# A pool of 160 bytes and a gap of 192 bytes that move the weights and the tokens to another distance in SBUF

## The chip, the cores and the metric

The kernel runs on one core of one Trainium2 chip. The metric is the device time of one execution in microseconds (us). Before the change it is 1328.35 us, the median of three runs (1327.24 to 1328.72).

## What is computed

One layer of a streaming encoder for 288 tokens (256 of a prompt and 32 of a running stream, D_MODEL 2048), all in float32:

```
xn   = rmsnorm(x);  proj = xn @ w_in               # 2048 x 5664
pool = trailing means of u_pool, times w_pool      # 4 groups of 256 x 256
ssd  = SSD mixer (conv, chunked scan, gate, norm)
x    = x + rmsnorm(concat[pool, ssd] @ w_out)      # 3072 x 2048
h    = rmsnorm(x) @ w_up                           # 2048 x 11264
f    = silu(conv(gate)) * conv(value)
x    = x + rmsnorm(f @ w_down)                     # 5632 x 2048
```

The new states of the mixers and of the convolutions are outputs too.

## The kernel before, in words

**Products.** Weights are the stationary operand, tokens the moving one. Both are split into a high and a low float32r part. A block of 128 x 128 weights with one token tile takes three matmuls, in `mm3` (lines 141 to 144): high weights with high tokens (L142), high weights with low tokens (L143), low weights with high tokens (L144). Each has 288 moving columns, and each is preceded by a load of its weights. One "product" below is one such load and matmul, a "triple" the three of `mm3`.

**Token tiles.** A token tile is `[128, 2, 288]` float32r: per partition 1152 bytes of high part, then 1152 bytes of low part. 1152 is 4 x 256 + 128, so the low part lies at 128 bytes (mod 256) from the high part, and one tile of 2304 bytes is 9 x 256, so all tiles of a pool have the same address mod 256.

**Weights.** `project` (L146) runs a stage: `fetch_w` (L117) issues the DMA of up to 1 MB into a `raw` tile of `wpool`, `split_w` (L124) makes `whi` on ScalarE (L136) and `wlo` on VectorE (L137), 4096 bytes each per partition, also in `wpool`. A weight block begins at a multiple of 512 bytes within them, so all weights of `wpool` have one address mod 256. The first stage alone (`prepare`, L270 and L359) has its split weights in a tile `w` of the pool `xin`.

**The stages**, in the order of time, and the token tiles that they read:

| stage | us of the span | token tile, pool | triples |
|---|---|---|---|
| first part of w_in (L359) | 4 to 39 | `xn`, apool | 96 |
| rest of w_in | 47 to 310 | `xn`, apool | 608 |
| w_pool | 296 to 333 | `du`, outp | 16 |
| w_out, SSD part | 312 to 456 | `mixs`, apool | 256 |
| w_out, pool part | 340 to 469 | `mixp0` to `mixp7`, outp | 128 |
| w_up, both halves | 475 to 755, 897 to 1176 | `hn`, apool | 1408 |
| w_down, both halves | 756 to 897, 1176 to 1299 | `fa`, ffn | 660 |
| last 256 columns of w_down (L1262, L1263, L1285) | 1299 to 1318 | `fa`, ffn | other shapes |

In between stand a few small products: the sums over features (L690, L891: the weights are the tile `ones_r` of ones), the SSD heads (L631 to L637), the new states (L972, L973, 512 columns).

**Pools.** Tile pools are laid out in SBUF one behind the other in the order in which they are opened: const, wpool, apool, bpool, upool, and behind these xin, then mixer, then outp, then ffn, each in the place of the one that was closed. Every tile is rounded up to 32 bytes per partition.

**Order.** The scheduler sets the order of the instructions on each engine from its own estimates; many are pinned to the program's order.

Of the kernel before, what the change touches and what calls it, by code (L numbers as in the profile page):

```python
# [8 lines left out]
F32 = mybir.dt.float32  # L9
# [7 lines left out]
P = 128  # L17
# [8 lines left out]
HEADS = 32  # L26
# [4 lines left out]
NF = D_FF // P  # L31
# [19 lines left out]
)  # L51
SUMS_AT = 11
TURN_AT = 13
NEAR = 8


@with_exitstack
def body(
# [24 lines left out]

    const = ctx.enter_context(tc.tile_pool(name="const", bufs=1))
    wpool = ctx.enter_context(tc.tile_pool(name="wpool", bufs=4))
    apool = ctx.enter_context(tc.tile_pool(name="apool", bufs=16))
    bpool = ctx.enter_context(tc.tile_pool(name="bpool", bufs=20))
    acc_ps = ctx.enter_context(tc.tile_pool(name="acc_ps", bufs=5, space=PSUM))
# [135 lines left out]
    first_load(9)  # L224
    cols = const.tile([P, sum(n for _, n in COLS)], F32, name="cols")
    pin(sp.dma_start(out=cols, in_=cols_in))
    hp = const.tile([HEADS, 3], F32, name="hp")
    pin(sp.dma_start(out=hp, in_=heads_in))
    col = {}
    for name, n in COLS:  # L230
# [2 lines left out]

    ones = const.tile([P, P], F32, name="ones")
    pool.memset(ones, 1.0)
    eps_t = const.tile([P, 1], F32, name="eps_t")
    pool.memset(eps_t, EPS)
    warm = const.tile([P, 1], F32, name="warm")
    pin(act.activation(warm, eps_t, AF.Copy))
    ident = const.tile([P, P], F32, name="ident")  # L240
    make_identity(nc, ident)
# [1 line left out]
    pool.affine_select(  # L243
        out=tri, in_=ones, pattern=[[1, P]], compare_op=ALU.is_ge, fill=0.0, base=0, channel_multiplier=-1
    )
    rec = const.tile([P, 16], F32, name="rec")
    for t in range(16):
        pool.memset(rec[:, t : t + 1], 1.0 / (t + 1))
    scan_one = const.tile([HEADS, NT], F32, name="scan_one")
# [224 lines left out]
    def htile(name, n=NT, tag=None):  # L474
        return mp.tile([HEADS, n], F32, tag=tag or name, name=name, bufs={"z": 4}.get(tag, 2) if tag else 1)
# [23 lines left out]
    r = htile("r", tag="z")  # L499
# [355 lines left out]

    xT = op_.tile([P, NEAR, NT], F32, name="xT2")
    x1 = []
# [146 lines left out]
    for grp in ((0, 1), (2,), (3,), (4,), (5,), (6, 7)):  # L1004
# [13 lines left out]
        if grp[0] == 0:  # L1018
            sp.dma_start(out=xT.rearrange("p k n -> p (k n)"), in_=x_g[:, KD : KD + NEAR * NT])
            sp.dma_start(out=new_sconv, in_=sc_stage.rearrange("p s r t -> p (s r t)"))  # L1020
# [15 lines left out]
    def hn_of(t):  # L1036

        a = atile("hn")
        hi = act.activation(a[:, 0, :], x1[t], AF.Copy, scale=g_ffn_pre[:, t : t + 1])  # L1039
        lo = pin(dve.scalar_tensor_tensor(  # L1040
            a[:, 1, :], x1[t], g_ffn_pre[:, t : t + 1], a[:, 0, :].bitcast(F32),
            op0=ALU.mult, op1=ALU.subtract,
        ))
        if t == 0:
            late.extend((hi, lo))
        q = xsum if t == 0 else op_.tile([P, NT], F32, tag="sq", bufs=2, name="sq")
        act.activation(q, x1[t], AF.Square)
        hn.append(a)
        if t == 1:
            state_out(*still)  # L1050
        if t:
            squares[t] = q
        if t > 1:
            pin(dve.tensor_tensor(xsum, xsum, squares.pop(t - 1), op=ALU.add))

    todo = list(range(KD))
    for s in range(KD):
        pin(dve.tensor_tensor(x1[s], x1[s], rm, op=ALU.mult))
        if s < NEAR:
            pin(dve.tensor_tensor(x1[s], x1[s], xT[:, s, :], op=ALU.add))  # L1060
        else:
            pin(pool.dma_start(out=x1[s], in_=x_g[:, KD + NT * s : KD + NT * (s + 1)], accum_op=ALU.add))
        while todo and todo[0] + (1 if todo[0] < NEAR else NEAR) <= s:
            hn_of(todo.pop(0))
# [9 lines left out]

    ffn = ExitStack()
    fp = ffn.enter_context(tc.tile_pool(name="ffn", bufs=1))
    fc_stage = fp.tile([P, 2, 2, 2 * NF], F32, name="fc_stage")
    nconv = [0]

    def fconv(i, p_):  # L1080
# [79 lines left out]
    for q in range(4):  # L1160
        for b in range(2):
            t = apool.tile([P, 512], F32, tag="a", name="xr")
# [31 lines left out]
    def factors(src, bias, n, name):  # L1194
        o = const.tile([P, 2], F32, tag="trs", bufs=2, name=name)[:, :n]
        pin(act.activation(o, src, AF.Sqrt, bias=bias, scale=1.0 / D_MODEL))
        pin(dve.reciprocal(o, o))
        return o
# [53 lines left out]
    def turn(t):  # L1252
        c = slice((t - A) * P, (t - A + 1) * P)
        pin(pe.transpose(last[:, 2 * P + c.start : 2 * P + c.stop], part[t][:, P:NP_], ident))
        pin(pe.matmul(last_s[P - NS :, c], part[t][:, NP_:], ident, start=True, stop=True))
# [27 lines left out]
    for k, hi, lo in sum(parts, []):  # L1283
# [4 lines left out]
        if k == SUMS_AT:  # L1288
            other_sums(sq[0], False)
            rf = factors(p_f, eps_t, 2, "rf1")  # L1290
        if k == TURN_AT:
            turn(A)
# [108 lines left out]
```

## Time and profile before

| what | value |
|---|---|
| median of 3 runs | 1328.35 us |
| the profiled execution, its own time | 1328.16 us |
| its span, first to last instruction | 1326.4 us |
| granted TensorE clock | 1.000 |
| DVE (VectorE), ACT (ScalarE), POOL (GpSimd) busy | 67%, 51%, 19% |
| largest DMA group, w_up | 80 of 1 MB, 5.1 us to landing |

How to read it: the page gives for each engine the busy share of the span, then the chain of work that ended last, then groups of instructions. Matmuls overlap in the record: a product of 288 columns is shown with about 295 ns, but the next one starts about 132 ns later. So the pace is read from starts, or from the number of products in a stretch. The stretches of the windows view count every instruction that touches the stretch, the two or so that were under way at its start among them.

### The profile page before, as it was taken

The page shows a single profiled execution, that of the slowest core. Times are in us where ns is not written, and L with a number is a line of the kernel's source. Part 1 is how long each engine was busy: PE and PEld are TensorE (multiplying, and loading weights), DVE is VectorE, ACT ScalarE, POOL GpSimd, SP SyncE. Part 2 cuts the span into 40 slices and gives each one's busy share as a digit, 9 for nine tenths or more (in the row PEclk, how much of TensorE's full clock was granted, in tenths as well). Part 3 has the DMA queues.
Part 4 walks back from the last instruction along what each step waited for, and adds up shares of the span by engine and source line. Part 5 has one row for each costly group of instructions (what it writes and reads, how often), then busy time and mean ns, then how long its engine had stood idle before and what let it go on. Part 6 is the DMA issues. An engine that isn't in the chain of part 4 may idle for free.

```text
span 1326.4 us, 25268 instructions
## 1 busy us (share of the span) xinstructions
PE 1319.0 (99%) x10043; PEld 1307.9 (99%) x10043; DVE 894.3 (67%) x1515; ACT 672.5 (51%) x1013; POOL 247.5 (19%) x399
## 2 busy tenths in 40 slices
PE   9999999999999999999999999999999999999998
PEld 9999999999999999999999999999999999999997
DVE  7999987879645688876766743336666666654454
ACT  7557767446543567544444433334444454444442
POOL 2342222222232231211211200001111111101110
PEclk9999999999999999999999999999999999999999
DMA  8578875456566478666455444545444544466653
GB/s 340 183 216 280 280 215 177 155 169 208 198 210 223 138 196 264 198 176 205 160 162 175 157 161 165 164 166 180 167 159 162 178 169 160 162 231 181 209 177 114
DMA packets 110038, 251.75 MB, mean 190 GB/s; under 512 B 64736, under 2 KB 73856, under 8 KB 87392
## 3 DMA queue, kind: packets, MB, share of 16 engines
q1 hardware_dynamic: 103424, 233.22, 54.2%
q0 software_dynamic: 5824, 16.13, 4.2%
q8 instruction: 78, 1.28, 0.4%
q10 hardware_dynamic: 672, 0.80, 0.2%
q14 instruction: 40, 0.33, 0.1%
HBM read 237.11 MB, written 13.00 MB: 189 GB/s over the span
## 4 chain that ended last, share of the span: by engine, by line
PE 98%; DMA 0%; ACT 0%; DVE 0%; issue 0%; ACTq 0%
PE acc L142 30%; PE acc L144 30%; PE acc L143 30%; PE acc L359 2%; PE acc_x L359 1%; PE py L631 1%; PE acc L1262 0%; DMA xg<-in_x_g 0%; PE acc L1263 0%; PE acc_t L1285 0%; PE acc_x L143 0%; PE acc_x L142 0%; PE acc_x L144 0%; PE py L633 0%; PE pst L972 0%; PE acc L366 0%
## 5 line engine op out<-in xcount | busy, mean ns | idle before, releaser
L137 DVE TENSOR_TENSOR wlo<-raw,whi 128x1024 fp32r<-128x1024 f32 (+1 forms) x396 | 472.8, 1195 | 321.0 <-ACT whi L136 319.2
L136 ACT ACTIVATE whi<-raw 128x1024 fp32r<-128x1024 f32 (+1 forms) x396 | 408.3, 1033 | 486.2 <-PE acc L143 401.3
L142 PE MATMUL acc<-hn,whi 128*128 128x288 f32 x1376 | 404.6, 296 | 0.5 <-ACT hn L1039 0.4
L143 PE MATMUL acc<-hn,whi 128*128 128x288 f32 x1376 | 403.4, 294 | 0.0
L144 PE MATMUL acc<-hn,wlo 128*128 128x288 f32 x1376 | 403.0, 294 | 0.0
L143 PEld LDWEIGHTS acc<-hn,whi 128*128 128x128 f32 x1376 | 259.7, 189 | 0.1
L144 PEld LDWEIGHTS acc<-hn,wlo 128*128 128x128 f32 x1376 | 259.5, 189 | 0.0
L142 PEld LDWEIGHTS acc<-hn,whi 128*128 128x128 f32 x1376 | 257.2, 187 | 1.4 <-ACT hn L1039 0.8
L143 PE MATMUL acc<-fa,whi 128*128 128x288 f32 x660 | 195.4, 296 | 0.0
L142 PE MATMUL acc<-fa,whi 128*128 128x288 f32 x660 | 195.3, 296 | 0.0
L144 PE MATMUL acc<-fa,wlo 128*128 128x288 f32 x660 | 195.0, 295 | 0.0
L142 PE MATMUL acc<-xn,whi 128*128 128x288 f32 x608 | 180.1, 296 | 0.0
L144 PE MATMUL acc<-xn,wlo 128*128 128x288 f32 x608 | 178.8, 294 | 0.0
L143 PE MATMUL acc<-xn,whi 128*128 128x288 f32 x608 | 178.8, 294 | 0.0
L143 PEld LDWEIGHTS acc<-fa,whi 128*128 128x128 f32 x660 | 124.4, 188 | 0.0
L142 PEld LDWEIGHTS acc<-fa,whi 128*128 128x128 f32 x660 | 124.0, 188 | 0.0
L144 PEld LDWEIGHTS acc<-fa,wlo 128*128 128x128 f32 x660 | 123.8, 188 | 0.0
L1088 POOL COPY fc_stage<-ebuf 128x4 f32<-128x4 f32 x88 | 26.7, 304 | 483.7 <-DVE ebuf L1087 462.2
L143 PEld LDWEIGHTS acc<-xn,whi 128*128 128x128 f32 x608 | 114.9, 189 | 0.0
L144 PEld LDWEIGHTS acc<-xn,wlo 128*128 128x128 f32 x608 | 114.7, 189 | 0.1
L142 PEld LDWEIGHTS acc<-xn,whi 128*128 128x128 f32 x608 | 113.9, 187 | 0.7 <-issue 0.5
L1094 DVE SCALAR_TENSOR_TENSOR fc<-ebuf,cols,fc 128x290 f32<-128x290 f32 x176 | 90.1, 516 | 3.7 <-ACT fc L1092 1.0
(338 smaller groups left out, 1778.4 us busy)
## 6 DMA issues: line engine op xcount, KB each, us to landing
raw<-in_w_up SPq DMA_DIRECT2D x80, 1024.0 KB, 5.1
raw<-in_w_in SPq DMA_DIRECT2D x38, 1024.0 KB, 5.2
raw<-in_w_down SPq DMA_DIRECT2D x32, 1024.0 KB, 5.0
raw<-in_w_out SPq DMA_DIRECT2D x24, 1024.0 KB, 5.1
raw<-in_w_down SPq DMA_DIRECT2D x16, 768.0 KB, 4.4
raw<-in_w_up SPq DMA_DIRECT2D x14, 512.0 KB, 4.1
gb<-g_d POOLq DMA_DIRECT2D x8, 832.0 KB, 6.0
raw<-in_w_first SPq DMA_DIRECT2D x5, 768.0 KB, 12.6
```

The source lines that it names most:

```text
L136: act.activation(hi, raw[:, k : k + n, :], AF.Copy)
L137: dve.tensor_tensor(lo, raw[:, k : k + n, :], hi.bitcast(F32), op=ALU.subtract)
L142: then(pe.matmul(out, wh, a[:, 0, :], start=start, stop=False))
L143: then(pe.matmul(out, wh, a[:, 1, :], start=False, stop=False))
L144: then(pe.matmul(out, wl, a[:, 0, :], start=False, stop=stop))
L359: pin(pe.matmul(first[m], w[:, k, r * NB + m * P :][:, :P], xn[kb + k][:, x, :], start=kb + k + r + x == 0, stop=kb + k == KD - 1 and r == ...
L631: ins = pe.matmul(y[c, 0:256], xw[:, 0, f_], m[:, h, 0:256], start=True, stop=False)
L1088: pool.tensor_copy(fc_stage[:, :, :, i], e[:, 256:324].rearrange("p (s c) -> p s c", c=34)[:, :, 0:2])
L1094: dve.scalar_tensor_tensor(c, e[:, r_ : r_ + 290], f_w[:, r_, i : i + 1], c, op0=ALU.mult, op1=ALU.add)
```

## The change

Four small tiles (`hp`, `eps_t`, `warm`, `rec`; 32 + 32 + 32 + 64 = 160 bytes with the rounding) leave the pool `const`, which lies ahead of `wpool`, for a new pool `side`, which lies behind it and ahead of `apool`. And `fc_stage`, the first tile of the pool `ffn`, becomes the front part of a tile that is 48 floats (192 bytes) longer.

```diff
+FC_GAP = 48
...
     wpool = ctx.enter_context(tc.tile_pool(name="wpool", bufs=4))
+    side = ctx.enter_context(tc.tile_pool(name="side", bufs=1))
     apool = ctx.enter_context(tc.tile_pool(name="apool", bufs=16))
...
-    hp = const.tile([HEADS, 3], F32, name="hp")
+    hp = side.tile([HEADS, 3], F32, name="hp")
...
-    eps_t = const.tile([P, 1], F32, name="eps_t")
+    eps_t = side.tile([P, 1], F32, name="eps_t")
...
-    warm = const.tile([P, 1], F32, name="warm")
+    warm = side.tile([P, 1], F32, name="warm")
...
-    rec = const.tile([P, 16], F32, name="rec")
+    rec = side.tile([P, 16], F32, name="rec")
...
-    fc_stage = fp.tile([P, 2, 2, 2 * NF], F32, name="fc_stage")
+    fc_room = fp.tile([P, 8 * NF + FC_GAP], F32, name="fc_stage")
+    fc_stage = fc_room[:, : 8 * NF].rearrange("p (s r t) -> p s r t", s=2, r=2)
```

Both programs have the same instructions in the same order on every engine; they differ in addresses. `wpool` begins 160 bytes earlier, at 34624 instead of 34784; apool, bpool, upool, xin, mixer and outp stay where they were; what lies behind `fc_stage` in ffn begins 192 bytes later. Addresses in SBUF mod 256, and the distance token minus weight (high part / low part):

| stage | weights, before / after | tokens, before / after | distance before | distance after |
|---|---|---|---|---|
| first part of w_in | 160 / 160 | 224 / 224 | 64 / 192 | 64 / 192 |
| rest of w_in, w_pool, w_out SSD part, w_up | 224 / 64 | 224 / 224 | 0 / 128 | 160 / 32 |
| w_out, mixp0 to mixp3 | 224 / 64 | 96 / 96 | 128 / 0 | 32 / 160 |
| w_out, mixp4 to mixp7 | 224 / 64 | 224 / 224 | 0 / 128 | 160 / 32 |
| w_down | 224 / 64 | 32 / 224 | 64 / 192 | 160 / 32 |

`ones_r`, in const behind the tiles that left, moves from 64 to 160; the tokens of L891 lie at 96 and 224 in both.

## The prediction

> **What bounds the kernel now.** First the page: its busy shares, its clock row and its chain of work.
>
> ```profile
> span 1326.4 us, 25268 instructions
> PE 1319.0 (99%) x10043; PEld 1307.9 (99%) x10043; DVE 894.3 (67%) x1515; ACT 672.5 (51%) x1013; POOL 247.5 (19%) x399
> ...
> PEclk9999999999999999999999999999999999999999
> ...
> PE 98%; DMA 0%; ACT 0%; DVE 0%; issue 0%; ACTq 0%
> PE acc L142 30%; PE acc L144 30%; PE acc L143 30%; PE acc L359 2%; PE acc_x L359 1%; PE py L631 1%; PE acc L1262 0%; DMA xg<-in_x_g 0%; PE acc L1263 0%; PE acc_t L1285 0%; PE acc_x L143 0%; PE acc_x L142 0%; PE acc_x L144 0%; PE py L633 0%; PE pst L972 0%; PE acc L366 0%
> ```
>
> TensorE is busy for 99% of the span at the full granted clock, and 98% of the chain that ended last is TensorE, nine tenths of it in the three lines of `mm3`. Then the view of waits, for TensorE; its two longest entries:
>
> ```profile
> PE acc_x L265 <- DVE busy L192: 1.3, 1, 1.3
> PE acc L359 <- ACT w L294: 0.7, 1, 0.7
> ```
>
> Nobody keeps it waiting. The order of instructions is the same in both programs, so only one thing can move the time: how long a product takes from its start to the next start. The durations of single matmuls (295 ns) overlap, so I count products in long stretches that hold one stage each: the windows view, with the stretch, then TensorE's busy time and its instructions.
>
> ```profile
> core 0: us, PE busy (x) PEld busy (x) DVE busy (x) ACT busy (x) POOL busy (x), PEclk, DMA share, GB/s
> ...
> 50.00:105.00 55.00, 55.00 (x418) 55.00 (x418) 53.91 (x121) 28.09 (x42) 24.16 (x24) 1.00 0.62 186
> 560.00:740.00 180.00, 180.00 (x1363) 180.00 (x1362) 123.21 (x221) 84.57 (x114) 30.29 (x56) 1.00 0.55 173
> 760.00:890.00 130.00, 130.00 (x977) 130.00 (x976) 51.20 (x50) 48.17 (x61) 1.20 (x1) 1.00 0.51 169
> 900.00:1170.00 270.00, 270.00 (x2044) 270.00 (x2043) 178.31 (x313) 126.67 (x170) 47.53 (x82) 1.00 0.50 166
> ```
>
> About 2.2 products were under way at the start of a stretch (295 ns over 132). Without them w_in (50 to 105) gives 55,000/415.8 = 132.3 ns per product, w_up 180,000/1360.8 = 132.3 and 270,000/2041.8 = 132.2, w_down 130,000/974.8 = 133.4. The shape is the same everywhere. DVE is busy for 98% of the w_in stretch and 39% of the w_down one, and yet w_down is the slower: the load beside TensorE isn't the cause. What differs is the distance between tokens and weights: 0/128 bytes in w_in and w_up, 64/192 in w_down. I use 132.25 and 133.35.
>
> **Is it the distance, or the place of the tokens alone?** The first part of w_in has its tokens where the rest of w_in has them (224), and weights at 160: distance 64/192. The timeline, with start, length, line and count:
>
> ```profile
> 28.93 1.76 PE L359 MATMUL acc_x<-xn,w 128*128 128x288 f32 x12
> 30.53 3.36 PE L359 MATMUL acc<-xn,w 128*128 128x288 f32 x24
> 33.73 1.76 PE L359 MATMUL acc_x<-xn,w 128*128 128x288 f32 x12
> ```
>
> From 28.93 to 33.73 stand 36 products: 4.80/36 = 133.3 ns, the pace of w_down to the last digit, with tokens and weights both at other addresses than there. So the distance sets it. The third distance in this kernel is 128/0, at mixp0 to mixp3. Two of the eight passages over these tiles, from the second triple to the end, 21 products each:
>
> ```profile
> 347.24 0.30 PE L142 MATMUL acc<-mixp,whi 128*128 128x288 f32 x1
> ...
> 349.99 0.29 PE L142 MATMUL acc<-mixp,whi 128*128 128x288 f32 x1
> ```
> ```profile
> 386.91 0.30 PE L142 MATMUL acc<-mixp,whi 128*128 128x288 f32 x1
> ...
> 389.69 0.29 PE L142 MATMUL acc<-mixp,whi 128*128 128x288 f32 x1
> ```
>
> 2.75/21 = 131.0 ns, and 2.78/21 = 132.4. Seven passages go like the first and one like the second: the pace is one of a few fixed ones, and what came before can decide which.
>
> **A rule of the skill that speaks against the change.** The rows above differ by 2.4 ns with the distance. The Trainium skill, page "TensorE: Matmul & The Clock Gate", section "Step-by-step: what each phase is for", says that TensorE has two independent read ports into SBUF, so that loading the next weights takes nothing from the running matmul. By that the distance would be without effect and the sum zero; the rows of w_in and L359 differ from it in the small, by 0.8%.
>
> **The change part by part.** *What is removed and added:* no instruction. *What moves:* `wpool` by 160 bytes, `fa` by 192. The split of weights reads and writes inside `wpool` alone, so its operands keep their distances; its two instructions end ahead of TensorE's need (the waits above name neither), and I cost them at nothing. The covers are DVE's idle time, which is 1.1 us of 55 in the stretch 50 to 105. A TensorE faster by 1% would meet DVE there at 99%; if it bound, up to 0.5 us of the gain of that stretch would be lost. The landing address of the weights' DMA moves as well; they land here in 5.1 us:
>
> ```profile
> raw<-in_w_up SPq DMA_DIRECT2D x80, 1024.0 KB, 5.1
> ```
>
> One such MB is two splits' worth of weights and feeds 48 products (6.3 us), and no wait of TensorE names a DMA: nothing.
>
> *The main products.* Their counts, from the page and from the groups kept apart by shape:
>
> ```profile
> L142 PE MATMUL acc<-hn,whi 128*128 128x288 f32 x1376 | 404.6, 296 | 0.5 <-ACT hn L1039 0.4
> ...
> L142 PE MATMUL acc<-fa,whi 128*128 128x288 f32 x660 | 195.3, 296 | 0.0
> ...
> L142 PE MATMUL acc<-xn,whi 128*128 128x288 f32 x608 | 180.1, 296 | 0.0
> ```
> ```profile
> L142 PE MATMUL acc<-mixs,whi 128*128 128x288 f32 x256 | 75.4, 295 | 0.0
> ...
> L142 PE MATMUL acc<-mixp,whi 128*128 128x288 f32 x128 | 37.8, 295 | 0.0
> ...
> L142 PE MATMUL acc_x<-hn,whi 128*128 128x288 f32 x32 | 9.1, 295 | 0.0
> ```
>
> From distance 0/128 to 160/32 go hn 1408, xn 608, mixs 256, half of mixp 64 and w_pool 16 triples: 2352, or 7056 products. From 64/192 to 160/32 go fa's 660 triples, 1980 products. From 128/0 to 32/160 go the other 64 of mixp, 192 products.
>
> *The pace at 160/32* stands in no long stretch. The bounds, by rows: the fewest nanoseconds are those of L1285, 256 columns.
>
> ```profile
> 1312.78 2.22 PE L1285 MATMUL acc_t<-whi,fa 128*128 128x256 f32 x18
> ```
>
> 18 products span 2.22 us, the last one alone some 0.28: 1.94/17 = 114 ns, or 128.5 for 288 columns if it went by columns. The most are those just behind a run of 512 columns, with distance 0/128:
>
> ```profile
> 373.78 0.30 PE L142 MATMUL acc<-mixs,whi 128*128 128x288 f32 x1
> ...
> 374.19 0.30 PE L142 MATMUL acc<-mixs,whi 128*128 128x288 f32 x1
> ```
>
> 0.41/3 = 136.7 ns. Only four products have weights and tokens at 32 and 160 now, the sums of L891, and they too follow on 512 columns:
>
> ```profile
> 470.09 0.29 PE L891 MATMUL psum_m<-mhi,ones_r 128*128 128x288 f32 x1
> 470.22 0.29 PE L891 MATMUL psum_m<-mlo,ones_r 128*128 128x288 f32 x1
> 470.36 0.30 PE L891 MATMUL psum_m<-mhi,ones_r 128*128 128x288 f32 x1
> 470.49 0.35 PE L891 MATMUL psum_m<-mlo,ones_r 128*128 128x288 f32 x1
> ```
>
> Three starts in 0.40 us, 133 ns, against the 0.41 us of distance 0/128 in the same position. The starts are rounded to 0.01 us, so this says little: not worse than 0/128, and no sign of 128. In the circle of 256 bytes, two of three products of a triple go to 160, which is 32 from 128 (the best row, 131.0) and 96 from 0 and from 64. I take the nearest row, **131.0**.
>
> Sum: 7056 x (132.25 - 131.0) = 8.8 us; 1980 x (133.35 - 131.0) = 4.7 us; the 192 products of mixp0 to mixp3 go the other way, to 32, between 0 and 64, at (132.25 + 133.35)/2 = 132.8: 192 x 1.8 = 0.35 us lost. The last 132 products of w_down have other shapes; at 1 to 2 ns each they are 0.2 us, left out. Together 13.1 us less. From the profiled execution's 1328.16 us that gives 1315.1, and the median stands 0.2 above it: **1315 us**, 1.0% less.
>
> **The rivals.**
>
> *Slower: 160 behaves as 64 does.* Then all stages go at the pace of w_down: 7056 x 1.1 = 7.8 us more, 192 x 2.35 = 0.45 more, 1336.6. For it: two of the four distances seen pairwise (64 and 192) are bad, the weights now begin at another place within 64 bytes than the tokens, which no long stretch shows, and L891 gave 133. Against: 160 lies nearer to 128. It decides from a pace of (7056 x 132.25 + 1980 x 133.35 + 192 x 131.0)/9228 = 132.5 ns on: above that the change loses.
>
> *No effect, or 160 behaves as 0.* If the distance has no part in it, 1328. If 160 is as 0, only w_down gains, 1980 x 1.1 = 2.2 us: 1326. For it: the best distance, 128, went at 132.4 in one passage, as 0 does. Its first half is the skill's rule above; the rows of L359 speak against that half.
>
> *Much faster: 160 avoids what all three others still pay.* At the lower bound, 128.5: 7056 x 3.75 + 1980 x 4.85 + 192 x 2.5 = 36.5 us less, 1292. For it: one step of 64 bytes moves the pace by 1 ns already, and none of the three distances is an odd multiple of 32. Against: L891.
>
> **How the numbers follow.** Nearest row, 1309 to 1322: 0.34. Much faster, down to 1292: 0.24. No effect or as 0, 1323 to 1330: 0.14. Slower, 1331 and above: 0.28, mostly up to 1337; beyond that only if 160 is worse than all that is seen (136.7 would be some 40 us more). Below 1292 and above 1337 I leave 0.05 and 0.12, so the range is 1292 to 1337. A measurement of this kernel tells about 0.2% (2.7 us) from no change. Faster by more: 0.34 + 0.24 and a little of the third case, 0.60. Within 0.2%: 0.13. Slower: 0.27.
>
> **What would show it.** In the windows view of the changed kernel the stretches inside w_up and w_down must have the same pace now, both having 160/32: at 131.0 ns 180 us hold 1376 products, against 1363. If they are equal but at 133, the slower rival is right; if w_down keeps a pace of its own, it isn't the distance that set it. L359 keeps 64/192 and must keep its 133.3. The chain stays TensorE's; a wait of TensorE for `whi` or `wlo` between 50 and 105 us would show that DVE's cover is gone. All of it is wrong if the pace depends on which cycle a stage falls into at its start rather than on the distance: then equal distances would show unequal paces.

## The result

| | before | changed |
|---|---|---|
| median of 5 runs each | 1328.35 us | 1322.35 us (1321.8 to 1322.48) |
| ratio, with 95% interval | | 0.9955 [0.9940, 0.9969] |
| profiled execution, own time | 1328.16 us | 1322.35 us |
| its span | 1326.4 us | 1320.6 us |

The kernel became 6.0 us faster (0.45%). The forecast was 13.1 us (1315), with a range of 1292 to 1337. The sign holds; the size is less than half. After the change the page reads as before: the same instructions, TensorE busy throughout at the full clock, and the chain of work nine tenths in the three lines of `mm3` (now L144 to L146). Only the head of the chain differs: up to 38.7 us it goes over the DMA and the split of the first weights, where it went over L359 before.

```profile
span 1320.6 us, 25268 instructions
PE 1313.9 (99%) x10043; PEld 1302.5 (99%) x10043; DVE 894.7 (68%) x1515; ACT 672.5 (51%) x1013; POOL 251.8 (19%) x399
...
PEclk9999999999999999999999999999999999999999
...
PE 96%; DMA 1%; DVE 1%; ACT 1%; issue 0%; SPq 0%; ACTq 0%
```

In the view of waits TensorE's list still names neither `whi` nor `wlo`; its longest three entries:

```profile
PE acc_x L267 <- DVE busy L194: 1.3, 1, 1.3
PE py__15330 L1330 <- ACT diag L1329: 0.7, 1, 0.7
PE acc L144 <- ACT hn L1041: 0.4, 1, 0.4
```

The windows view of the changed kernel, the same stretches as in the prediction:

```profile
50.00:105.00 55.00, 55.00 (x419) 55.00 (x418) 53.99 (x122) 28.47 (x41) 24.97 (x24) 1.00 0.63 186
560.00:740.00 180.00, 180.00 (x1367) 180.00 (x1366) 122.67 (x221) 84.92 (x113) 33.36 (x56) 1.00 0.56 175
760.00:890.00 130.00, 130.00 (x988) 130.00 (x987) 50.79 (x48) 48.81 (x60) 0.00 (x0) 1.00 0.50 167
900.00:1170.00 270.00, 270.00 (x2050) 270.00 (x2049) 178.93 (x314) 126.78 (x170) 47.48 (x82) 1.00 0.51 169
```

Less the 2.2 that were under way, w_up ran 1364.8 products in 180 us (131.9 ns each; before 132.3) and w_down 985.8 in 130 us (131.9; before 133.4). The two stages have one pace now, but the stretch from 560 to 740 shows 1367 products where 131.0 ns would have shown 1376. The first part of w_in, whose distance didn't change, stands in the timeline:

```profile
32.87 1.76 PE L361 MATMUL acc_x<-xn,w 128*128 128x288 f32 x12
34.47 2.70 PE L361 MATMUL acc<-xn,w 128*128 128x288 f32 x19
```

12 products from 32.87 to 34.47: 1.60/12 = 133.3 ns, as before.

Counts in a window are good to one product. Where more digits are given below, the pace is the time between the starts of the first and the last product of an unbroken stretch of the trace, over their number. By that measure the 5.8 us of the span come from:

| products | distance | ns per product, before to after | us |
|---|---|---|---|
| w_up (hn), 4224 | 0/128 to 160/32 | 132.23 to 131.85 | -1.6 |
| w_in, rest (xn), 1824 | 0/128 to 160/32 | 132.25 to 131.94 | -0.6 |
| w_out, mixs, 768 | 0/128 to 160/32 | 132.33 to 131.50 | -0.6 |
| w_out, mixp4 to mixp7, 192 | 0/128 to 160/32 | 132.21 to 131.24 | -0.2 |
| w_out, mixp0 to mixp3, 192 | 128/0 to 32/160 | 131.37 to 133.31 | +0.4 |
| w_down (fa), 1980 | 64/192 to 160/32 | 133.33 to 131.86 | -2.9 |

Together -5.5 us. The first part of w_in, with the same distance, ends 0.3 us earlier; that is inside the scatter of the program's head, since the rest of w_in begins anywhere from 46.4 to 48.2 us in the kept traces. The middle rows already hold a question: mixs and w_up have the same distances, 160/32, and not the same pace.

### The profile page after: what moved, and what is told of

Same layout as the page of the kernel before. It is cut to its first block, busy times and chain, and to the rows that moved or that the text cites. A ratio compares the mean times of both kernels' runs of the same rounds, so it can differ in the third digit from the quotient of the medians.

```text
span 1320.6 us, 25268 instructions
## 1 busy us (share of the span) xinstructions
PE 1313.9 (99%) x10043; PEld 1302.5 (99%) x10043; DVE 894.7 (68%) x1515; ACT 672.5 (51%) x1013; POOL 251.8 (19%) x399
## 4 chain that ended last, share of the span: by engine, by line
PE 96%; DMA 1%; DVE 1%; ACT 1%; issue 0%; SPq 0%; ACTq 0%
PE acc L145 30%; PE acc L144 30%; PE acc L146 30%; DMA raw<-in_w_first 1%; PE py L633 1%; PE acc L1265 0%; DVE w L300 0%; PE acc L1266 0%; PE acc_t L1288 0%; PE acc_x L145 0%; PE acc_x L144 0%; PE acc_x L146 0%; DVE sq L320 0%; PE py L635 0%; PE acc L361 0%; PE acc_x L361 0%
## 5 line engine op out<-in xcount | busy, mean ns | idle before, releaser
L146 PE MATMUL acc<-hn,wlo 128*128 128x288 f32 x1376 | 404.5, 295 | 0.0
L144 PE MATMUL acc<-hn,whi 128*128 128x288 f32 x1376 | 402.9, 294 | 0.5 <-ACT hn L1041 0.4
L144 PEld LDWEIGHTS acc<-hn,whi 128*128 128x128 f32 x1376 | 258.8, 189 | 1.4 <-ACT hn L1041 0.8
L146 PEld LDWEIGHTS acc<-hn,wlo 128*128 128x128 f32 x1376 | 258.3, 188 | 0.0
L146 PE MATMUL acc<-fa,wlo 128*128 128x288 f32 x660 | 194.6, 295 | 0.0
L144 PE MATMUL acc<-fa,whi 128*128 128x288 f32 x660 | 194.0, 294 | 0.0
L146 PE MATMUL acc<-xn,wlo 128*128 128x288 f32 x608 | 179.5, 296 | 0.0
L144 PE MATMUL acc<-xn,whi 128*128 128x288 f32 x608 | 179.4, 295 | 0.0
L144 PEld LDWEIGHTS acc<-fa,whi 128*128 128x128 f32 x660 | 124.5, 189 | 0.0
L146 PEld LDWEIGHTS acc<-fa,wlo 128*128 128x128 f32 x660 | 123.9, 188 | 0.0
L144 PEld LDWEIGHTS acc<-xn,whi 128*128 128x128 f32 x608 | 114.6, 189 | 0.7 <-issue 0.5
L146 PEld LDWEIGHTS acc<-xn,wlo 128*128 128x128 f32 x608 | 114.2, 188 | 0.1
L1086 POOL COPY ebuf<-cols 128x2 f32<-128x2 f32 x88 | 74.0, 842 | 108.7 <-DVE fc L1097 61.2
```

What stands on the lines that cost most here:

```text
L144: then(pe.matmul(out, wh, a[:, 0, :], start=start, stop=False))
L146: then(pe.matmul(out, wl, a[:, 0, :], start=False, stop=stop))
L1086: pool.tensor_copy(e[:, 258:260], hist_f[:, :, i])
```

## Experiments

### One part of the change at a time, and the place without the distance

Theory "distance": only the distance between tokens and weights (mod 256) counts. Rival "place": the address of the weights or of the tokens alone counts. `side_only` is the change without the gap in `fc_stage` (w_down then lies at 224/96); `gap_only` is the gap without the side pool (w_down then lies at 0/128 and all else as before).

> The side pool alone, no gap in ffn: w_in, w_out and w_up at distance 160/32 (weights at 64 mod 256), w_down at 224/96, a pair not seen yet. Theory 'distance' (the pace depends on token minus weight mod 256): w_up at 131.85 ns per product as after the change, which is 7056 x 0.4 = 2.8 us less than before; w_down anywhere from 130 to 134 ns, a pace of its own: 1325.5 us with up to 7 us either way. Theory 'place' (it is the weights' own address, 64 instead of 224, that helps): w_down at 131.85 as well, 1322.4 us.

> The gap alone, no side pool: weights at 224, w_down at distance 0/128, everything else as before. Theory 'distance': w_down takes the pace of w_up, 132.25 instead of 133.35 ns, 1980 x 1.1 = 2.2 us less: 1326.2 us. Theory 'place' (the weights' own address): nothing changes, 133.35 ns in w_down and 1328.35 us.

`abs96` puts 96 bytes in front of everything: weights and tokens move together, no distance changes, and the weights begin at 64 as in the changed kernel.

```diff
+    const.tile([P, 24], F32, name="gap")
```

> 96 bytes at the head of the pool const: weights at 64 mod 256 as after the change, but the tokens move with them, so all distances are those of before (0/128 and 64/192). Theory 'distance': 132.25 ns in w_up, 133.35 in w_down, 1328.35 us. Theory 'place': w_up and w_down at 131.85, 1322.4 us.

`pad128` puts 128 bytes between `wpool` and `apool`: 128/0 for w_in and w_up, 192/64 for w_down. It asks whether the 131.0 ns of the prediction's row at 128/0 hold in a long stage.

```diff
     wpool = ctx.enter_context(tc.tile_pool(name="wpool", bufs=4))
+    gap = ctx.enter_context(tc.tile_pool(name="gap", bufs=1))
+    gap.tile([P, 32], F32, name="gap")
```

> 128 bytes between wpool and apool: w_in, w_out and w_up at 128/0, w_down at 192/64. This is the row that the prediction took for the pace, in a whole stage. If the seven fast passages over mixp0 to mixp3 are the rule: 131.0 ns in w_up, 7056 x 1.25 = 8.8 us less, 1319.5 us if w_down keeps its pace. If a long stage settles in the cycle of the eighth passage: 132.4 ns in w_up, about 1 us more, 1329.4 us. w_down at 192/64 is open, 131 to 134 ns.

| kernel | us (runs) | ratio to before | w_up | w_down |
|---|---|---|---|---|
| side_only | 1323.75 (6) | 0.9971 [0.9959, 0.9983] | 160/32: 131.85 | 224/96: 133.33, then 132.23 |
| gap_only | 1325.74 (10) | 0.9985 [0.9976, 0.9995] | 0/128: 132.22 | 0/128: 132.22 |
| abs96 | 1327.37 (10) | 0.9998 [0.9988, 1.0007] | 0/128: 132.23 | 64/192: 133.33 |
| pad128 | 1325.22 (10) | 0.9979 [0.9970, 0.9989] | 128/0: 132.22 | 192/64: 132.59 |

One stretch of w_up and one of w_down in the windows view of each; first `abs96`:

```profile
560.00:740.00 180.00, 180.00 (x1364) 180.00 (x1363) 122.89 (x221) 85.05 (x113) 31.21 (x56) 1.00 0.55 173
770.00:880.00 110.00, 110.00 (x827) 110.00 (x826) 43.01 (x38) 41.87 (x52) 0.00 (x0) 1.00 0.50 168
```

1364 and 827 products; the kernel before has 1363 and 827 in these stretches. The place alone does nothing, and "place" falls. `gap_only`:

```profile
560.00:740.00 180.00, 180.00 (x1363) 180.00 (x1362) 122.57 (x221) 85.11 (x113) 32.51 (x56) 1.00 0.56 173
770.00:880.00 110.00, 110.00 (x834) 110.00 (x833) 43.39 (x38) 42.22 (x53) 0.00 (x0) 1.00 0.50 169
```

Only w_down changed, to 834 - 2.2 products in 110 us, 132.2 ns: the pace that w_up has at the same 0/128. `side_only`, with a second stretch of w_down:

```profile
560.00:740.00 180.00, 180.00 (x1367) 180.00 (x1366) 123.23 (x222) 85.10 (x114) 33.36 (x57) 1.00 0.56 176
770.00:880.00 110.00, 110.00 (x827) 110.00 (x826) 43.40 (x38) 41.57 (x52) 0.00 (x0) 1.00 0.50 168
...
1190.00:1285.00 95.00, 95.00 (x720) 95.00 (x720) 47.16 (x56) 42.06 (x57) 12.64 (x11) 1.00 0.66 197
```

w_up has the pace of the changed kernel without the gap. But w_down runs its first half at 133.4 ns (824.8 products in 110 us) and its second at 132.4 (717.8 in 95 us), with the same distance 224/96. So the distance doesn't name one pace; it allows some. `pad128` shows the same thing in w_in. Its group of first products in the window from 60 to 95 us, then w_up:

```profile
L144 PE MATMUL acc<-xn,whi 128*128 128x288 f32 x90 | 26.6, 295 | 0.0
```
```profile
59.91 0.30 PE L144 MATMUL acc<-xn,whi 128*128 128x288 f32 x1
...
94.92 0.29 PE L144 MATMUL acc<-xn,whi 128*128 128x288 f32 x1
```
```profile
560.00:740.00 180.00, 180.00 (x1363) 180.00 (x1363) 122.78 (x221) 85.01 (x113) 30.91 (x56) 1.00 0.55 172
```

90 triples from 59.91 to 94.92 are 89 x 3 products in 35.01 us: 131.1 ns. The interruption of the stream by small products at 106 to 109 us ends that: behind it the triples (from the start of one to the start of the next, read from the trace in ns) go 395, 398, 395, 399, which is 132.2 ns a product; another interruption, at 199 us, brings 389, 397, 394 back. And w_up, at the same 128/0, runs 1360.8 products in 180 us, 132.3 ns, to its end. The row that the prediction rested on is thus one of two paces of 128/0, and the time of `pad128` lies between the two that were expected.

### High and low tokens by themselves

Theory "own": the pace of a triple is the sum of what each product's own distance costs. In these kernels all three products of `mm3` read the high tokens, or all three the low ones, so that a stage has one distance only (half of the tokens' parts is left out, so what they compute isn't the layer); `pure_0` and `pure_128` stand on the kernel before, `pure_160` and `pure_32` on `side_only`.

```diff
-        then(pe.matmul(out, wh, a[:, 1, :], start=False, stop=False))
+        then(pe.matmul(out, wh, a[:, 0, :], start=False, stop=False))
```
```diff
-        then(pe.matmul(out, wh, a[:, 0, :], start=start, stop=False))
+        then(pe.matmul(out, wh, a[:, 1, :], start=start, stop=False))
...
-        then(pe.matmul(out, wl, a[:, 0, :], start=False, stop=stop))
+        then(pe.matmul(out, wl, a[:, 1, :], start=False, stop=stop))
```

> The layout of before, but the second product of every triple reads the high part of the tokens again: the low part is left out of the result, and all three products have one distance, 0 in w_in, w_out and w_up, 64 in w_down. Theory 'own' (each product pays for its own distance, and a triple is the sum): from the pairs seen so far, 0/128 at 396.7 ns per triple and 128/0 at 396.7, 64/192 at 400 and 192/64 at 397.8, follow 132.2 ns per product for 0 and 134.1 for 64. Theory 'cycle' (the stream of loads and products falls into one of a few fixed cycles that the distances allow, and no product has a price of its own): any of the paces seen, 131.1 to 133.3, and no need to be 134.1 at 64.

> The layout of before with the low part of the tokens in all three products (the high part is left out of the result): distance 128 alone in w_in, w_out and w_up, 192 alone in w_down. 'Own': 132.2 ns for 128 and 131.85 for 192. 'Cycle': 131.1 or 132.2 for 128, 192 open.

> The side pool without the gap, high part of the tokens in all three products (the low part is left out of the result): distance 160 alone in w_in, w_out and w_up, 224 alone in w_down. 'Own': from 160/32 at 395.6 and 32/160 at 399.9 ns per triple follow 130.4 ns for 160, the best of all. 'Cycle': one of 131.1 or 131.85 again. 224 alone: open, as the pair 224/96 went at 133.3 in one half and 132.2 in the other.

> The side pool without the gap, low part of the tokens in all three products (the high part is left out of the result): distance 32 alone in w_in, w_out and w_up, 96 alone in w_down. 'Own': 134.8 ns for 32; for 96 from 224/96 somewhere in 131 to 136. 'Cycle': 131 to 133.3 for both.

One profiled run each, 1320.84, 1335.82, 1334.62 and 1333.04 us beside 1327.82 before. w_up in the windows views of `pure_0`, `pure_160` and `pure_32`:

```profile
560.00:740.00 180.00, 180.00 (x1369) 180.00 (x1369) 123.52 (x223) 85.36 (x115) 32.07 (x57) 1.00 0.56 175
```
```profile
560.00:740.00 180.00, 180.00 (x1353) 180.00 (x1352) 122.65 (x222) 84.28 (x112) 32.76 (x57) 1.00 0.56 174
```
```profile
560.00:740.00 180.00, 180.00 (x1353) 180.00 (x1352) 123.51 (x225) 85.01 (x114) 30.98 (x56) 1.00 0.56 173
```

0 alone runs at 131.7 ns; 160 alone and 32 alone both run at 133.3 (1350.8 products in 180 us), and yet 160 and 32 by turns run at 131.85. "Own", which wanted 130.4 for 160 alone, falls: what counts is how the distances follow on one another. By starts, the others alone: 64 at 132.22 or 131.67, 96 at 131.67, and 128, 192 and 224 at 133.33.

### The other distances

`pad32` and `pad96` are `pad128` with 8 and with 24 floats (w_in and w_up at 32/160 and at 96/224; w_down at 96/224 and at 160/32).

> 32 bytes between wpool and apool: w_in, w_out and w_up at 32/160, w_down at 96/224. Theory 'cycle' (a pair of distances allows one or a few fixed cycles): 32/160 was 133.3 ns over mixp0 to mixp3 after the change, so w_up at 133.3 and 7056 x 1.1 = 7.8 us more; w_down at 96/224 open, 131.7 to 133.3, up to 3.3 us less: 1333 to 1336 us, slower than before. Theory 'any odd multiple of 32 helps': 131.9 in both, 1323 us.

> 96 bytes between wpool and apool: w_in, w_out and w_up at 96/224, w_down at 160/32 with the weights still at 224. 'Cycle' and 'distance': w_down at 131.85 ns as after the change, 3.0 us less than before; 96/224 open: 224/96 went at 133.3 or 132.2, 96 alone at 131.7, so w_up 131.7 to 133.3 and 1321 to 1333 us.

`pad32` took 1335.01 us (4 runs), 1.0052 [1.0035, 1.0068], with 133.33 ns nearly everywhere; `pad96` 1331.76 (6), 1.0031 [1.0019, 1.0043]. The rows of `pad96`:

```profile
560.00:740.00 180.00, 180.00 (x1352) 180.00 (x1352) 122.40 (x222) 84.30 (x112) 32.51 (x57) 1.00 0.56 174
770.00:880.00 110.00, 110.00 (x836) 110.00 (x836) 43.38 (x38) 40.61 (x51) 0.00 (x0) 1.00 0.49 164
```

Its w_down has the changed kernel's distance, 160/32, by another way (weights at 224, tokens at 128), and the changed kernel's pace: 110,000/833.8 = 131.9.

### What makes w_out faster than w_up at the same distance

In the changed kernel most rounds of 32 triples of mixs run faster than w_up. The first and last of one round:

```profile
391.93 0.29 PE L144 MATMUL acc<-mixs,whi 128*128 128x288 f32 x1
...
404.12 0.29 PE L144 MATMUL acc<-mixs,whi 128*128 128x288 f32 x1
```

31 triples in 12.19 us: 131.1 ns. The lengths of the triples tell two repeating patterns apart: 393, 393, 394 ns here, 391, 391, 404.5 in w_up. Ahead of this round go the tiles mixp0 to mixp3 at 32/160, and mixp4 to mixp7 at 160/32, already in the faster pattern. The one later round without mixp ahead of it, at 372.9 us behind the 512 columns of the new states, has the pattern of w_up, though its tiles and its distance are the same. Theory "entry": coming out of 32/160 puts the stream into the faster pattern. Then the kernel whose mixp0 to mixp3 lie at 160/32 too must lose it:

```diff
             if g == 0 and kb == 0:
+                op_.tile([P, 32], F32, name="gap")
                 pool_group(1)
```

> The changed kernel with mixp0 to mixp3 moved by 128 bytes, so that all of w_out has the distance 160/32 and nothing at 32/160 runs any more. Theory 'entry': w_out never leaves the slower cycle, 131.85 ns in mixs and mixp instead of 131.5 and 131.2 (0.4 us more over 960 products), while the 192 products of mixp0 to mixp3 go from 133.3 to 131.85 (0.3 us less): the time stays at 1322.4 us and only the paces tell. Theory 'w_out itself': mixs stays at 131.5 or less, and mixp0 to mixp3 join it at 131.2.

1322.09 us (7 runs), 0.9965 [0.9954, 0.9976]. A round of mixs in it:

```profile
351.63 0.30 PE L144 MATMUL acc<-mixs,whi 128*128 128x288 f32 x1
...
363.90 0.29 PE L144 MATMUL acc<-mixs,whi 128*128 128x288 f32 x1
```

31 triples in 12.27 us, 131.9 ns: the faster pattern is gone, "entry" holds. What the kernel loses there it gains at mixp0 to mixp3 (133.3 to 131.8), so its time is that of the changed kernel.

If so, a few products at 32/160 put into w_up must move the rest of the program into the faster pattern. The kernels `kick` add some to the changed kernel, into an accumulator that nobody reads, at the start of the pass of w_up with `j == 4` (525 us). `kick4` and `kick5` add four and five triples at its very start (the same loop, ahead of the first `mm3`); `kick4_at1`, `kick4_at2` and `kick4_at3` add four triples behind its first one, two and three triples (`k == 1`, `2`, `3`). The main lines of `kick4_at2`, without those that hand `kick` on:

```diff
                             for k, hi, lo in part:
+                                if kick and i + m0 + q + m == 0 and k == 2:
+                                    p_ = aux([P, NT], "kick")
+                                    for r in range(3 * kick):
+                                        pin(pe.matmul(p_, hi[:, :P], acts[k][:, 1 - (r % 3) % 2, :], start=r == 0, stop=r == 3 * kick - 1))
...
-                    up(((0, j, 2),))
+                    up(((0, j, 2),), kick=4 if j == 4 else 0)
```

> The changed kernel with 12 more products at distances 32/160/32 into an unused accumulator, at the start of the fourth pass of w_up (about 520 us into the span); the result is unchanged. Theory 'entry' (at 160/32 there are two cycles, 131.1 and 131.85 ns, and what ran just before decides which; w_out found the fast one behind mixp0 to mixp3): this or the run with 15 products finds the fast cycle and keeps it to the end, about 1940 triples x 3 x 0.74 ns = 4.3 us less, 1.6 us paid for the 12: 1319.6 us. The other one stays at 131.85 and takes 1324 us. Theory 'place in the program' (w_out is fast for another reason, its tiles or its DMA load): both stay at 131.85, 1324 us.

> The same with 15 products. Theory 'entry': fast cycle in this run or in the one with 12, 1320.0 us with it (4.3 us less, 2.0 us paid), 1324.4 without. Theory 'place in the program': 131.85 ns, 1324.4 us.

> The same behind the first triple: the stream stands at 391, 404, as in the one passage over mixp0 to mixp3 that did not lead to the fast cycle. 'Entry': 131.85 ns, 1324 us. 'w_out itself': the same.

> The changed kernel with 12 products at 32/160/32 into an unused accumulator in the fourth pass of w_up, behind its second triple. 'Entry': in the runs kick4 and kick5 the added products stood behind two short triples (391, 391) and fell into a cycle of 400, 400; over mixp0 to mixp3 the stream came from 404, 391, ran 402, 398, 402, 398 and then found the fast cycle. Behind the second triple the stream should stand at 404, 391: the added triples run near 402, 398, 402, 398 and w_up and w_down follow at 131.1 ns, about 4.3 us less for 1.6 paid, 1319.6 us. 'w_out itself': 131.85, 1324 us.

> The same behind the third triple: the stream stands at 391, 391 again, as in kick4. 'Entry': 131.85 ns, 1324 us. 'w_out itself': the same.

| kernel | us (runs) | lengths of the added triples, ns | w_up and w_down behind them |
|---|---|---|---|
| kick4 | 1323.51 (6), 0.9968 [0.9957, 0.9980] | 400, 399, 400, 400 | 131.85 |
| kick5 | 1324.45 (8), 0.9973 [0.9963, 0.9984] | 399, 399, 400, 400, 400 | 131.85 |
| kick4_at1 | 1324.0 (1) | 399, 400, 397, 403 | 131.85 |
| kick4_at2 | 1319.91 (4), 0.9944 [0.9929, 0.9959] | 402, 397, 403, 397 | 131.11 |
| kick4_at3 | 1323.15 (1) | 400, 399, 400, 400 | 131.85 |

`kick4` and `kick5` ran first, and neither did what was expected of one of them. From the triples in their traces came the expectations of the three others, and these held: two went by unnoticed, and `kick4_at2`, expected at 1319.6 us, did what was looked for. Its timeline around the added products:

```profile
526.80 1.76 PE L174 MATMUL kick<-hn,whi 128*128 128x288 f32 x12
528.40 0.29 PE L144 MATMUL acc<-hn,whi 128*128 128x288 f32 x1
...
529.97 0.29 PE L144 MATMUL acc<-hn,whi 128*128 128x288 f32 x1
```

The 12 added products take 1.60 us (133.3 ns each), the 12 behind them 1.57 (131), and so it goes on to the end, through w_down:

```profile
560.00:740.00 180.00, 180.00 (x1375) 180.00 (x1374) 123.45 (x221) 85.50 (x115) 29.85 (x56) 1.00 0.55 173
770.00:880.00 110.00, 110.00 (x841) 110.00 (x840) 43.77 (x39) 42.98 (x53) 0.00 (x0) 1.00 0.52 171
```

1375 products in w_up's 180 us against 1367, with the same distances: within one product the 1376 that the prediction had named. 32/160 has two patterns of its own, 400, 400 and 402, 397. Behind the even one, and behind a 403, the stream falls back to 131.85; behind a short triple (397) it goes to 131.11. The same holds in w_out of the changed kernel: of eight passages over mixp0 to mixp3, the seven that end on a short triple (397 or 398) enter the faster pattern and the one that ends on 403 doesn't. And it holds in `pad32`, where mixs lies at 32/160 and mixp0 to mixp3 at 160/32: of its eight passages into 160/32 the six behind a 397 or 398 go 394, 393, 393, and the two behind an even 400 fall into 391, 391, 404.

`kick2_at2` asks whether two triples do as well as four.

```diff
-                    up(((0, j, 2),), kick=4 if j == 4 else 0)
+                    up(((0, j, 2),), kick=2 if j == 4 else 0)
```

> As kick4_at2 with 6 products instead of 12: two triples, 402 and 397. 'Entry': it is the short triple at the end that counts, so w_up and w_down follow at 131.1 ns and the time is 0.8 us below kick4_at2, about 1319.1 us. If the stream needs the two rounds to settle: 131.85 ns and 1323.2 us.

1318.81 us (4 runs, 1318.22 to 1320.35), 0.9932 [0.9916, 0.9949], the fastest of all: six useless products (402, 397) are enough, as the theory wanted. The times against the kernel before don't tell it from the changed kernel beyond their intervals, but the traces do: from the first product of w_up to the end of the span the changed kernel takes 846.9 us, `kick4_at2` 844.2 and `kick2_at2` 843.8, 3.1 less. Its windows:

```profile
560.00:740.00 180.00, 180.00 (x1375) 180.00 (x1374) 123.40 (x221) 86.36 (x116) 29.81 (x56) 1.00 0.55 173
770.00:880.00 110.00, 110.00 (x841) 110.00 (x841) 43.40 (x38) 42.83 (x53) 0.00 (x0) 1.00 0.51 169
```

## Why the prediction was right in sign and wrong in size

- **"only one thing can move the time: how long a product takes from its start to the next start": right.** Same instructions, no new wait, and the paces by stage add up to 5.5 of the 5.8 us.
- **"So the distance sets it": right, but not all of it.** `abs96` (distances kept, 0.9998 [0.9988, 1.0007]) against `side_only` and `gap_only` shows that the place has no part. `side_only` and the kicks show that one distance can have two paces.
- **"I take the nearest row, 131.0": this step failed.** The pace of 160/32 in the long stages is 131.85, so that 7056 products brought 3.0 us instead of 8.8, and the 1980 of w_down 2.9 instead of 4.7. The row was a short passage of 128/0 in one of its two paces; w_up at 128/0 runs at 132.2 in `pad128`. The prediction had quoted the second passage, 132.4, and left it out of the sum. And near in the circle of 256 bytes doesn't mean near in pace: 160 alone runs at 133.3, 0 alone at 131.7. So the sign was partly luck: the choice of 131.0 by nearness had no ground, and at the 133.3 of 32/160, the same two distances with the shares exchanged, the change would have lost (the prediction's own limit was 132.5).
- **None of the rivals came true:** 160/32 went neither as 64 (133.3) nor as 0 (132.2) nor at the lower bound (128.5, which comes out of its row as 128.4).
- **192 products lost 0.35 us: right**, 0.37. Their pace came out at 133.3 instead of 132.8, and they had been at 131.4 rather than 131.0.
- **The rule of the Trainium skill.** By two independent read ports, where loading weights takes nothing from the running matmul (the Trainium skill, "TensorE: Matmul & The Clock Gate", "Step-by-step: what each phase is for"), the distance would do nothing. The traces disagree with that by up to 2.2 ns in 133, as w_down before (133.33) and behind the kick (131.11) show, with no wait of TensorE between.
- **Covers: right.** DVE at 53.99 of 55 us still kept nobody waiting, and no wait of TensorE names a DMA.
- **The named way to be wrong came true in part,** that "equal distances would show unequal paces": w_out and w_up at 160/32, the halves of w_down in `side_only`, w_in and w_up in `pad128`. The distance allows a few paces; the way in chooses one (shown for 160/32, by `mixp_moved`, `pad32` and the kicks; argued for the others), and it is kept until the stream is interrupted or its distance changes.

**What stays open:** what in the chip makes the paces; no run here shows it. The rule of the short triple was not tried beyond the passages and kicks above, and only distances that are multiples of 32 bytes were. That 128 bytes aren't the period is seen in 0 alone (131.7) and 128 alone (133.3); that 256 are was taken for granted.

## What to carry to other kernels

When TensorE alone bounds a kernel, as here with a weight load for every 288 columns, try the address of its moving operand against that of its weights, mod 256: moving a pool of 160 bytes and a buffer by 192 was worth 0.45%, and between the best and the worst distance tried lie 1.0% of the time (1322.35 and 1335.01 us). Take a pace from a stage as long as the one that you forecast; a pace from a short passage can be one that the long stage doesn't keep. And where the same shape at the same distance shows two paces, look at what the stream came from: a few products more can cost less than they bring. No other kernel was measured for any of this.

## What the runs showed that was not expected

The paces in ns per product of 288 columns, by distance (high/low, two of three products at the high one):

| 0/128 | 32/160 | 64/192 | 96/224 | 128/0 | 160/32 | 192/64 | 224/96 |
|---|---|---|---|---|---|---|---|
| 132.22 | 133.33 | 133.33 | 133.33 | 132.22, 131.1 | 131.85, 131.11 | 132.59 | 133.33, 132.23 |

Every pace in the table and in the `pure` kernels is 133.33 or lies a simple part of a twentieth of it (6.67 ns) below: less 1/9 (132.59), 1/6 (132.22), 2/9 (131.85), 1/4 (131.67) or 1/3 (131.11). This is arithmetic on the measured paces; why it is so isn't known. The triples repeat in patterns of two to four, and a pattern is carried over from w_up into w_down. Added work made the kernel faster: with 1.6 us of it in `kick4_at2`, measured side by side, 1319.91 us against 1322.09 for `mixp_moved` (which takes the changed kernel's time) and 1324.0 and 1323.15 for the same work one triple earlier or later.
